# A two-block sequence model on one core: the residual stream held token-major instead of channel-major

## The chip, the cores and the metric

The kernel runs on one core of one Trainium2 chip, in a single launch. The metric is the device time of that launch in microseconds (us), lower is better. Runs of the kernel before the change took 2954.91, 2952.97 and 2952.49 us; their median is 2952.97 us.

## The reference

The input x has 512 tokens of 1024 channels in float32. Eight stages follow each other; every one takes the residual stream x, normalises it, computes a mixer or a feed-forward part of it, and adds the result to x:

```python
for i in range(2):                       # first block
    h = rmsnorm(x, norm_mix_pre[i])
    m = ssd_mixer(h, ...) if i == 0 else rglru_mixer(h, ...)
    x = x + rmsnorm(m, norm_mix_post[i])
    h = rmsnorm(x, norm_ffn_pre[i])
    x = x + rmsnorm(conv_ffn(h, ...), norm_ffn_post[i])
...                                      # second block: even mixer, ffn, latent attention, ffn
```

`rmsnorm(x, w)` is x * rsqrt(mean(x^2 over the 1024 channels) + 1e-6) * w, per token. `conv_ffn` is an up product, a causal depthwise convolution along the tokens, a gate and a product back to 1024 channels; its inner width is 4096 in the first block and 2816 in the second. `ssd_mixer` (state-space, 2048 inner channels), `rglru_mixer` (gated linear recurrence, 1280 channels), the even mixer (HGRN2 and S5) and latent attention also begin with a product from 1024 channels and end with a product back to 1024. The second block adds its results without the norm behind (its stages have no post norm), and a last rmsnorm gives the output.

## The kernel before

**Layout.** x lies in eight tiles of 128 channels x 512 tokens (`x[k]`, L351). A product takes the weights as the stationary operand (128 x 128) and 512 tokens as the moving one. All products are made of two-part float32r values: a weight chunk and an activation are each split into a high and a low part, and `mm3` (L394) issues three matmuls, high-high, high-low and low-high. One output tile of 1024 inputs ("a unit", one weight chunk of eight blocks) is 24 matmuls of 512 columns (`proj`, L403).

**Weights.** Chunks are loaded by SP (`Weights.load`, L252), cast to the high part (`wh`, ScalarE or VectorE, L277 and L279) and the low part is the difference (`wl`, VectorE or GpSimd, L280), ahead of use, into pools of six buffers each.

**Norms.** `Entry.put` (L478) makes x * gain in two parts, not yet divided by the rms. The 1/rms of each token is `R`: squares on ScalarE (L426, L429), their sum over eight tiles on VectorE or GpSimd, a matmul with a matrix of ones that sums over the partitions (`inv_rms`, L442, the matmul is L447), logarithm, exponential and a Newton step. R is a 128 x 512 tile, and each unit's result is multiplied by it when it is taken out of PSUM: `pa<-mm,R`, `pb`, `cp`, `z`, `u`, `pr`, `t` and others, all at L392 (the helper `tt`). Convolutions then read that padded copy (`conv`, L631: one ScalarE instruction L634, then two or three VectorE instructions L636).

**The ends of stages.** The last product of a stage is taken together with the start of the next one. `post_end` (L527) ends the four stages that have a post norm (ssd, ffn0, lru, ffn1): the last product in halves of 256 tokens, the squares, R of each half, `newx` (L547: x += acc * R * gain, then `nxt.put`), and the first three units of the next stage in the same halves. GpSimd takes part in it (`nx` at L392, and `wl`, since L533 sets the plan "ag"). `res_end` (L581) ends even, ffn2 and mla: each output tile is added to x and put at once, and units begin while later tiles come. `final_end` (L594) ends ffn3 with the last norm and the output. After an end, up to three further units are taken into other PSUM banks until R of the entry is there (`ent.norm`).

**What sets the order.** A tile scheduler orders the instructions of each engine when the program is built; engines then run their queues in that order. `Flow` (L296) interleaves the tasks of a mixer. PSUM has three banks "mm" for units, and per stage two to five banks "ax", three "dn" in the feed-forward stages, two "y" in ssd.

## Time and profile before

| | |
|---|---|
| median of 3 runs | 2952.97 us (2952.49 to 2954.91) |
| profiled execution: span, first to last instruction | 2949.6 us |
| that span below the median of the runs | 3.4 us |
| TensorE (PE) busy | 2857.2 us, 97% of the span |
| VectorE (DVE) | 2098.5 us, 71% |
| ScalarE (ACT) | 1302.7 us, 44% |
| GpSimd (POOL) | 570.7 us, 19% |
| mean granted TensorE clock | 0.987 |
| chain that ended last | 83% PE, 12% DVE, 2% ACT |

The profile is of one execution; the page gives no time for it but the span, so the table sets that beside the median. "Busy" of PE counts matmuls whose modelled ends overlap the next one's start, so a full PE shows 74.00 of 74 us. PEld is the load of the stationary operand, which runs beside the matmuls. [...]

### The profile page before, as it was taken

The numbers are of one execution on the slowest core, as the hardware profiler recorded it, in microseconds if no ns is written. First come the engines' busy times: TensorE is split into PE (matmuls) and PEld (weight loads), VectorE is DVE, ScalarE is ACT, GpSimd is POOL, SyncE is SP. The second block draws the span as 40 slices with busy tenths as digits, with TensorE's granted clock in tenths as the row PEclk, the third lists the DMA queues.
The fourth block names the chain that finished last, engine by engine and source line by source line (L and its number), as shares of the span: only waits on it lengthen the run. The fifth ranks groups of instructions, "written<-read, shape, count | busy, mean of one in ns | idle before, by whom it ended". The sixth has DMA issues, their size and how long they took to land.

```text
span 2949.6 us, 36037 instructions
## 1 busy us (share of the span) xinstructions
PE 2857.2 (97%) x13264; PEld 2312.0 (78%) x13264; DVE 2098.5 (71%) x3346; ACT 1302.7 (44%) x2166; POOL 570.7 (19%) x751
## 2 busy tenths in 40 slices
PE   9999989999999879899999999999999999999998
PEld 7777778888888767778888877887888876788887
DVE  8987788666666996797767776676555576765555
ACT  5444446444333464553343344554333354443333
POOL 1323233000000544512432443101000010100000
PEclk9999999999999999999999999999999999999999
DMA  5122132222222122233333335622222221122222
GB/s 179 58 72 72 58 113 74 100 99 87 100 100 88 70 72 89 70 104 111 116 122 121 123 112 162 196 75 98 100 87 99 100 75 33 68 100 96 90 100 72
DMA packets 100639, 284.73 MB, mean 97 GB/s; under 512 B 19568, under 2 KB 30320, under 8 KB 99952
## 3 DMA queue, kind: packets, MB, share of 16 engines
q1 hardware_dynamic: 89824, 271.13, 26.9%
q10 hardware_dynamic: 10640, 11.30, 1.2%
q8 instruction: 105, 1.72, 0.2%
q14 instruction: 70, 0.57, 0.1%
HBM read 266.19 MB, written 16.22 MB: 96 GB/s over the span
## 4 chain that ended last, share of the span: by engine, by line
PE 83%; DVE 12%; ACT 2%; issue 1%; POOL 1%; DMA 1%; SPq 0%; DVEq 0%; POOLq 0%; ACTq 0%
PE mm L397 18%; PE mm L396 18%; PE mm L398 18%; PE dn L396 7%; PE dn L398 7%; PE dn L397 7%; DVE S L392 2%; DVE xl L485 2%; DVE x L551 1%; DVE wl L280 1%; PE ax L1700 1%; DVE co L636 1%; PE y L843 1%; PE ax L447 1%; PE ax L1722 1%
## 5 line engine op out<-in xcount | busy, mean ns | idle before, releaser
L277 ACT CAST wh<-raw 128x512 fp32r<-128x512 f32 x886 | 545.0, 620 | 1057.0 <-PE mm L397 658.8
L396 PE MATMUL mm<-xh,wh 128*128 128x512 f32 (+1 forms) x2440 | 941.1, 388 | 28.3 <-ACT xh L484 19.6
L397 PE MATMUL mm<-xl,wh 128*128 128x512 f32 (+1 forms) x2440 | 943.2, 387 | 18.8 <-DVE xl L485 18.8
L398 PE MATMUL mm<-xh,wl 128*128 128x512 f32 (+1 forms) x2440 | 938.8, 385 | 0.7 <-DVE wl L280 0.7
L280 DVE TENSOR_TENSOR wl<-raw,wh 128x512 fp32r<-128x512 f32 x822 | 600.6, 733 | 162.6 <-ACT wh L277 155.7
L396 PEld LDWEIGHTS mm<-xh,wh 128*128 128x128 f32 x2440 | 463.3, 191 | 123.2 <-ACT xh L484 22.0
L397 PEld LDWEIGHTS mm<-xl,wh 128*128 128x128 f32 x2440 | 464.8, 191 | 117.0 <-DVE xl L485 27.2
L398 PEld LDWEIGHTS mm<-xh,wl 128*128 128x128 f32 x2440 | 465.4, 191 | 91.3 <-issue 1.8
L396 PE MATMUL dn<-hsh,wh 128*128 128x512 f32 (+1 forms) x912 | 350.6, 384 | 0.1
L398 PE MATMUL dn<-hsh,wl 128*128 128x512 f32 (+1 forms) x912 | 349.4, 383 | 0.0
L397 PE MATMUL dn<-hsl,wh 128*128 128x512 f32 (+1 forms) x912 | 349.3, 383 | 0.0
L280 POOL TENSOR_TENSOR wl<-raw,wh 128x512 fp32r<-128x512 f32 x114 | 164.2, 1450 | 237.4 <-ACT wh L277 128.9
L396 PEld LDWEIGHTS dn<-hsh,wh 128*128 128x128 f32 x912 | 171.3, 188 | 37.8 <-issue 0.9
L398 PEld LDWEIGHTS dn<-hsh,wl 128*128 128x128 f32 x912 | 171.3, 188 | 37.0
L397 PEld LDWEIGHTS dn<-hsl,wh 128*128 128x128 f32 x912 | 171.4, 188 | 36.9
L636 DVE SCALAR_TENSOR_TENSOR ca<-pa,vec,ca 128x512 f32<-128x512 f32 x216 | 173.8, 805 | 37.0 <-ACT ca L634 31.3
L641 POOL MEMSET pa<- 128x2 f32 x108 | 10.4, 99 | 741.0 <-DVE ca L636 524.8
L392 DVE TENSOR_TENSOR acc<-dn,acc 128x512 f32<-128x512 f32 (+1 forms) x144 | 90.1, 628 | 76.7 <-PE dn L398 76.5
L392 DVE TENSOR_TENSOR x<-dn,x 128x512 f32<-128x512 f32 (+1 forms) x104 | 67.5, 650 | 105.2 <-PE dn L398 105.1
L392 DVE TENSOR_TENSOR pa<-mm,R 128x512 f32<-128x512 f32 x104 | 71.7, 690 | 75.6 <-PE mm L398 73.9
L634 ACT ACTIVATE ca<-pa,vec 128x512 f32<-128x512 f32 x108 | 88.2, 816 | 56.3 <-DVE pa L392 46.7
L410 ACT CAST hsh<-act 128x512 fp32r<-128x512 f32 x108 | 66.9, 620 | 100.5 <-DVE act L392 100.5
(512 smaller groups left out, 3767.1 us busy)
## 6 DMA issues: line engine op xcount, KB each, us to landing
raw<-w SPq DMA_DIRECT2D x233, 1024.0 KB, 4.8
sD<-s5t SPq DMA_DIRECT2D x4, 1024.0 KB, 5.7
sR<-s5t SPq DMA_DIRECT2D x4, 768.0 KB, 4.4
x<-xT SPq DMA_DIRECT2D x8, 256.0 KB, 5.8
kept<-x SPq DMA_DIRECT2D x8, 256.0 KB, 8.5
xo<-kept ACTq DMA_DIRECT2D x8, 256.0 KB, 3.0
s5t<-el ACTq DMA_DIRECT2D x8, 256.0 KB, 2.2
s5t<-HD ACTq DMA_DIRECT2D x4, 512.0 KB, 3.2
```

The source lines that it names most:

```text
L277: c.nc.scalar.copy(hi, r)
L280: (c.nc.gpsimd if e[1] == "g" else c.nc.vector).tensor_tensor(lo, r, hi.bitcast(F32), op=ALU.subtract)
L392: (eng or V).tensor_tensor(o, a, b, op=op)
L396: PE.matmul(ps, lhsT=wh, rhs=xh, start=first, stop=False)
L397: PE.matmul(ps, lhsT=wh, rhs=xl, start=False, stop=False)
L398: PE.matmul(ps, lhsT=wl, rhs=xh, start=False, stop=last)
L410: A.copy(hi, src)
L447: PE.matmul(ps[:, sl], lhsT=ones, rhs=s[:, sl], start=True, stop=True)
L485: V.scalar_tensor_tensor(lo[:, sl], x[k][:, sl], gk, hi[:, sl].bitcast(F32), op0=ALU.mult, op1=ALU.subtract)
L551: V.scalar_tensor_tensor(x[k][:, sl], t[:, sl], vc(gpost, k), (xo or x)[k][:, sl], op0=ALU.mult, op1=ALU.add)
L634: A.activation(o, src[:, nt - 1:], AF.Identity, scale=w[nt - 1], bias=b)
L636: V.scalar_tensor_tensor(o, src[:, j:j + T], w[j], o, op0=ALU.mult, op1=ALU.add)
```

## The change

x is now four tiles of 128 tokens x 1024 channels (a block of tokens each). The products back to 1024 channels take the activations as the stationary operand and 512 columns of weights as the moving one (`mmt`), so that their results are token-major; a last product is taken block by block of tokens, not in halves. The norm is along the free axis: `rms_rows` is two ScalarE squares with an accumulated sum (L494) and two GpSimd instructions on one column (L496, L497, a power of -1/2). `Entry.put` scales x by 1/rms (`n`, L513), transposes it on TensorE (eight 128 x 128 transposes per block, L516), and makes the two parts with the gain from PSUM (L521 on ScalarE, L522 on VectorE, eight of each per block). What the units give is then normed already: the multiplications by R are gone, and convolutions read PSUM directly. All seven inner ends are one function, `stage_end`, which takes three units of the next stage in halves; the first stage starts in the same way. The gain of a post norm is a row loaded by SP (`row`, L399). The pool of split weights has seven buffers.

```diff
+        def rms_rows(src):
+            ss = small.tile([P, 2], F32, name="ss", tag="ss")
+            for h in range(2):
+                A.activation(tmp("sq"), src[h], AF.Square, scale=1.0 / 32, accum_out=ss[:, h:h + 1])
+            rr = small.tile([P, 1], F32, name="rr", tag="rr")
+            G.tensor_scalar(rr, ss[:, :1], ss[:, 1:], EPS, op0=ALU.add, op1=ALU.add)
+            G.tensor_tensor(rr, rr, mhalf, op=ALU.pow)
+            return rr
...
-            def put(self, k, sl=FULL, square=True):
...
+            def put(self, q):
+                rr = rms_rows([half(x, q, h) for h in range(2)])
+                qs = slice(q * P, q * P + P)
+                for h in range(2):
+                    n = tmp("n")
+                    A.activation(n, half(x, q, h), AF.Identity, scale=rr)
+                    ps = mmps(c.tp)
+                    for e in range(4):
+                        PE.transpose(ps[:, e * P:e * P + P], n[:, e * P:e * P + P], ident)
+                    for e in range(4):
+                        hi, lo = self.xs[4 * h + e]
+                        gk = vc(self.gain, 4 * h + e)
+                        pe = ps[:, e * P:e * P + P]
+                        A.activation(hi[:, qs], pe, AF.Identity, scale=gk)
+                        V.scalar_tensor_tensor(lo[:, qs], pe, gk, hi[:, qs].bitcast(F32),
+                                               op0=ALU.mult, op1=ALU.subtract)
...
+        def mmt(ps, hk, q, w, first, last):
+            (hh, hl), (wh, wl) = hk, w
+            qs = slice(q * P, q * P + P)
+            PE.matmul(ps, lhsT=hh[:, qs], rhs=wh, start=first, stop=False)
+            PE.matmul(ps, lhsT=hh[:, qs], rhs=wl, start=False, stop=False)
+            PE.matmul(ps, lhsT=hl[:, qs], rhs=wh, start=False, stop=last)
...
         def down(name, hs, acc, first=None):
...
+            for h in range(2):
+                ws = parts_of(name, n)
+                for q in range(4):
+                    ps = mmps(c.dn)
+                    for k in range(n):
+                        mmt(ps, hs[k], q, ws[k], k == 0, k == n - 1)
...
+            def newx(q):
+                if g is not None:
+                    rr = rms_rows([half(acc, q, h) for h in range(2)])
+                    for h in range(2):
+                        t = tmp("nx")
+                        V.scalar_tensor_tensor(t, half(acc, q, h), rr, g[h],
+                                               op0=ALU.mult, op1=ALU.mult)
+                        tt(half(x, q, h), t, xo[2 * q + h] if xo else half(x, q, h), ALU.add)
+                nxt.put(q)
+            dn(0)
+            dn(1)
+            newx(0)
+            dn(2)
+            newx(1)
+            dn(3)
+            newx(2)
             uc = [W.next(u) for u in units]
             up = [mmps() for _ in units]
...
+            units_half(uc, up, nxt.xs, 0)
+            newx(3)
+            units_half(uc, up, nxt.xs, 1)
...
         def conv(name, src, nt, w, b):
...
-            A.activation(o, src[:, nt - 1:], AF.Identity, scale=w[nt - 1], bias=b)
+            A.activation(o, src, AF.Identity, scale=w[nt - 1], bias=b)
             for j in range(nt - 1):
-                V.scalar_tensor_tensor(o, src[:, j:j + T], w[j], o, op0=ALU.mult, op1=ALU.add)
+                d = nt - 1 - j
+                V.scalar_tensor_tensor(o[:, d:], src[:, :T - d], w[j], o[:, d:], op0=ALU.mult, op1=ALU.add)
...
             def convd(ps, ch, nm):
-                pad = padded("p" + nm, 3)
-                tt(pad[:, 2:], ps, r)
-                return conv("c" + nm, pad, 3, [vc(cw, t * nch + ch) for t in range(3)], vc(cb, ch))
+                return conv("c" + nm, ps, 3, [vc(cw, t * nch + ch) for t in range(3)], vc(cb, ch))
...
-                        pad = tmp("cp", 3 + T)
-                        A.copy(pad[:, :3], lneg[:, 3 * h:3 * h + 3])
-                        tt(pad[:, 3:], ps, r)
-                        o = conv("co", pad, 4, [vc("lcw", NH * t_ + h) for t_ in range(4)], lcb[:, h:h + 1])
+                        o = conv("co", ps, 4, [vc("lcw", NH * t_ + h) for t_ in range(4)], lcb[:, h:h + 1])
+                        tt(o[:, :3], o[:, :3], less[:, h], ALU.subtract)
...
+                if n == 0:
+                    warm_up()
+                    W.look = 0
+                    for q in range(4):
+                        ent.put(q)
+                        if q == 1:
+                            uc = [W.next("sin") for _ in range(3)]
+                            pre = [mmps() for _ in uc]
+                            units_half(uc, pre, ent.xs, 0)
+                    units_half(uc, pre, ent.xs, 1)
```

The order of instructions moves at three places.

ScalarE at the end of ffn0, the change: one block of tokens (`acc_4324` is the result of the second block, `x_82` and `x_83` are the first two blocks of x, `xh_4301` and so on are the high parts for the next stage).

```order
L494 ACTIVATE sq,ss<-acc_4323 128x512 x2
L494 ACTIVATE sq,ss<-x_82 128x512 x2
L283 CAST wh<-raw 128x512
L513 ACTIVATE n<-x_82,rr 128x512 x2
L494 ACTIVATE sq,ss<-acc_4324 128x512
L521 ACTIVATE xh_4301<-ax,vec 128x128
L521 ACTIVATE xh_4309<-ax,vec 128x128
L494 ACTIVATE sq,ss<-acc_4324 128x512
L521 ACTIVATE xh_4303<-ax,vec 128x128
L521 ACTIVATE xh_4311<-ax,vec 128x128
```

Before, ScalarE had there one square of 256 tokens and one `xh` per channel tile and half. Now each block has four squares, two scalings and eight small `xh` in its queue, and the next block's squares stand between them.

TensorE at the end of the even mixer, the change (`n_16759` and `n_16774` are the two halves of the first block's normed x; `ax_16743` is a half of the second block's last product, `ax_16789` of the third's, and `hsh`, `hsl` are the activations).

```order
L535 MATMUL ax_16743<-wl_16716,hsh_16523 128x512
L536 MATMUL ax_16743<-wh_16715,hsl_16524 128x512
L516 MATMUL ax_16761<-ident_104,n_16759 128x128 x4
L516 MATMUL ax_16776<-ident_104,n_16774 128x128 x4
L534 MATMUL ax_16789<-wh_16671,hsh_16411 128x512
L535 MATMUL ax_16789<-wl_16672,hsh_16411 128x512
```

The transposes of a block stand in TensorE's queue ahead of the last product of a later block, so that product waits until the earlier block is normed.

VectorE in the LRU mixer, where two heads' convolutions are taken out of PSUM; before and then the change.

```order
L392 TENSOR_TENSOR cp<-mm,R 128x512
L657 SCALAR_TENSOR_TENSOR spp<-spp,spq 128x10
L392 TENSOR_TENSOR cp<-mm,R 128x512
L657 SCALAR_TENSOR_TENSOR spp<-spp,spq 128x10
L279 CAST wh<-raw 128x512
L657 SCALAR_TENSOR_TENSOR spp<-spp,spq 128x10
L636 SCALAR_TENSOR_TENSOR co<-cp,vec,co 128x512
```

```order
L633 SCALAR_TENSOR_TENSOR co<-mm,vec,co 128x509
L285 CAST wh<-raw 128x512
L633 SCALAR_TENSOR_TENSOR co<-mm,vec,co 128x510
L633 SCALAR_TENSOR_TENSOR co<-mm,vec,co 128x509
L633 SCALAR_TENSOR_TENSOR co<-mm,vec,co 128x511
L633 SCALAR_TENSOR_TENSOR co<-mm,vec,co 128x510
L411 TENSOR_TENSOR co<-co,less 128x3
```

The multiplication by R is gone, the three convolution instructions read the PSUM bank `mm` themselves, and a small correction of three columns is added.

## Rows read from the trace of the kernel before

**Rows 1.** The page: span, busy time of TensorE, and the chain that ended last.

```profile
span 2949.6 us, 36037 instructions
...
PE 83%; DVE 12%; ACT 2%; issue 1%; POOL 1%; DMA 1%; SPq 0%; DVEq 0%; POOLq 0%; ACTq 0%
```

**Rows 2.** Stretch, length, busy PE, PEld, DVE, ACT, POOL; clock, DMA share, GB/s.

```profile
5.80:27.60 21.80, 18.94 (x74) 13.29 (x75) 18.97 (x28) 17.52 (x29) 4.37 (x7) 1.00 0.93 330
30.00:421.00 391.00, 379.58 (x1853) 292.82 (x1852) 328.37 (x493) 176.45 (x290) 105.71 (x105) 1.00 0.22 74
...
592.00:666.00 74.00, 74.00 (x325) 60.76 (x324) 50.01 (x74) 30.70 (x47) 0.89 (x9) 1.00 0.29 100
966.20:1010.00 43.80, 36.40 (x246) 34.29 (x246) 40.52 (x74) 24.35 (x53) 25.05 (x24) 0.84 0.13 49
1010.00:1188.00 178.00, 157.84 (x645) 124.14 (x644) 139.91 (x201) 88.64 (x133) 85.06 (x59) 0.95 0.24 83
...
1992.60:2016.70 24.10, 22.12 (x97) 17.95 (x97) 12.50 (x15) 9.01 (x15) 6.48 (x7) 1.00 0.27 93
...
2927.00:2949.60 22.60, 12.75 (x101) 12.04 (x100) 17.97 (x47) 8.24 (x20) 0.00 (x0) 0.87 0.28 94
```

**Rows 3.** TensorE's timeline in the post end of ffn0: start, duration, instruction, idle before.

```profile
966.26 0.28 PE L396 MATMUL dn<-hsh,wh 128*128 128x256 f32 x1
...
977.97 0.28 PE L398 MATMUL dn<-hsh,wl 128*128 128x256 f32 x1
980.73 0.91 PE L396 MATMUL mm<-xh,wh 128*128 128x256 f32 x3 [2.48 <-ACT xh L484]
...
982.50 0.41 PE L398 MATMUL mm<-xh,wl 128*128 128x256 f32 x1
```

**Rows 4.** TensorE's timeline in the res end of the even mixer and behind it.

```profile
1999.80 0.50 PE L397 MATMUL mm<-xl,wh 128*128 128x512 f32 x1 [1.98 <-DVE xl L485]
...
2016.52 0.39 PE L398 MATMUL dn<-xh,wl 128*128 128x512 f32 x1
2016.75 1.02 PE L447 MATMUL ax<-S,ones 128*128 128x512 f32 x2
```

**Rows 5.** TensorE's waits (us, count, longest) in ssd, 30 to 421, then lru, 1010 to 1188.

```profile
PE y L843 <- DVE sc L392: 5.2, 5, 1.4
...
PE mm L396 <- DVE cp L392: 7.7, 3, 4.4
PE ax L396 <- ACT xbh L410: 5.9, 3, 2.9
```

**Rows 6.** Groups of VectorE by line, 1010 to 1188 us: count, busy us, mean ns.

```profile
L636 DVE SCALAR_TENSOR_TENSOR co<-cp,vec,co 128x512 f32<-128x512 f32 x30 | 26.5, 899 | 0.0
...
L392 DVE TENSOR_TENSOR t<-mm,R 128x512 f32<-128x512 f32 x10 | 6.6, 679 | 0.0
...
L392 DVE TENSOR_TENSOR S<-S,sq 128x512 f32<-128x512 f32 x3 | 4.4, 1455 | 0.8 <-ACT sq L429 0.6
```

**Rows 7.** Groups of the whole trace by line and shape: what the new instructions are nearest to.

```profile
L484 ACT ACTIVATE xh<-x,vec 128x256 fp32r<-128x256 f32 x64 | 32.5, 507 | 50.3 <-DVE x L551 49.0 <-DMA sa<-s5a 1.2
...
L429 ACT ACTIVATE sq<-x 128x512 f32<-128x512 f32 x51 | 30.4, 618 | 0.0
...
L862 DVE SCALAR_TENSOR_TENSOR yy<-xc,vec,y 128x512 f32<-128x512 f32 x16 | 11.8, 740 | 0.0
...
L1442 DVE SCALAR_TENSOR_TENSOR st<-st,pr,ax 128x128 f32<-128x128 f32 x24 | 8.3, 345 | 0.9 <-ACT st L1440 0.5
...
L1706 ACT ACTIVATION_READ_ACCUMULATOR p<-ax,mx 128x1 f32 x32 | 6.2, 195 | 0.0
```

**Rows 8.** Small two-input instructions of GpSimd (lines); four transposes (TensorE's timeline).

```profile
L392 POOL TENSOR_TENSOR u<-tc,us 128x16 f32<-128x16 f32 x4 | 3.3, 824 | 0.3
...
L392 POOL TENSOR_TENSOR u<-ts,us 128x8 f32<-128x8 f32 x4 | 0.8, 204 | 0.0
...
50.11 0.60 PE L768 MATMUL ax<-ident,B 128*128 128x128 f32 x4
```

More of the change, by code (lines that the diff above doesn't have):

```diff
@@ L381, in build, with half, row @@
         FULL = slice(0, T)
+        def half(a, q, h):
+            return a[q][:, h * T:h * T + T]
+        def row(n):
+            out = [tmp("row") for _ in range(2)]
+            for h in range(2):
+                nc.sync.dma_start(out[h], aps["rows"][n:n + 1, h * T:h * T + T].to_broadcast([P, T]))
+            return out
         def tmp(name, w=T, dt=F32):
@@ L505, in down, with parts_of @@
+        def parts_of(name, n):
+            out = []
+            for _ in range(n // 2):
+                out += W.next(name).halves
+            return out
         def down(name, hs, acc, first=None):
             n = len(hs)
-            per = 8 // n
-            for j in range(KD):
-                if j % per == 0:
-                    ch = W.next(name)
-                ps = mmps(c.dn)
-                proj(ps, ch, hs, k0=(j % per) * n)
-                if first is None:
-                    tt(acc[j], ps, acc[j], ALU.add)
-                else:
-                    first(acc[j], ps, j)
-                yield n * 0.65, 0.0
@@ L520, in copy_first @@
-        def copy_first(a, ps, j):
+            for h in range(2):
+                ws = parts_of(name, n)
[3 more added lines that the diff above has]
+                        mmt(ps, hs[k], q, ws[k], k == 0, k == n - 1)
+                    if first is None:
+                        tt(half(acc, q, h), ps, half(acc, q, h), ALU.add)
+                    else:
+                        first(half(acc, q, h), ps, h)
+                    yield n * 0.69, 0.0
```

377 lines of the change are left out of this document (128 added, 249 removed).

## The prediction

> **What bounds the kernel now.** I read the page first, for the span, the busy shares and the chain that ended last [rows 1]: 83% of that chain is TensorE. Then the busy time by stretch [rows 2], because an average hides where TensorE is not full. In ffn0 it is busy 74.00 of 74 us at clock 1.00 while VectorE is busy 50.01: work taken off VectorE or ScalarE is worth nothing there, and this holds in all feed-forward stages. The reader should compare the other lines with it. ssd: TensorE lacks 391.00 - 379.58 = 11.4 us. lru: 178.00 - 157.84 = 20.2 us, and the clock is 0.95, another 178 x 0.05 = 9 us. A post end: 7.4 us of 43.8, at clock 0.84. A res end: 2.0 of 24.1. The output: TensorE is busy 12.75 of 22.6 us, so about 9.9 pass without it. What it waited for comes last: in lru mostly `cp` of VectorE and `xbh` of ScalarE, in ssd `sc` of VectorE [rows 5].
>
> So the change can gain in the interiors of ssd and lru and at the output, and can gain or lose at the start and at the seven ends between stages. The number of matmuls in the products stays what it is; 256 transposes come and the matmuls with `ones` go. The sum is made against the profiled span of 2949.6 us [rows 1], which is 3.4 below the median of the runs, 2952.97.
>
> **A post end, four times.** Before, it takes 43.8 us up to the first full-width unit [rows 2], and the norm's matmul between units costs about 1 us more [rows 4]: 44.8. In the change ScalarE gets a chain of small work for each block of 128 tokens: four squares with a sum, two scalings, eight `xh`. A 512-wide square takes 0.618 and a read of the accumulator 0.195 [rows 7]: 4 x 0.81 = 3.3. A scaling is taken like the square: 2 x 0.62 = 1.2. An `xh` of 128 columns isn't in the trace; it lies between the 128x1 at 0.195 and the 128x256 at 0.507 [rows 7]; I take 0.35, in between by width, so 2.8. That is 7.3 a block and 29 for four. Some five weight casts in the same queue, priced like the square, add 3. The queue begins when the first block's last product is done, a quarter of 11.7 us [rows 3], about 2.7 in. What it waits for is the chain of the first and of the last block: two pairs of GpSimd instructions on one column, VectorE's update of x, four transposes (0.60 [rows 8]). A 128x8 instruction of GpSimd takes 0.204 and a 128x16 one 0.824 [rows 8]; I take 0.4, nearer to the smaller since a column is smaller still, so 0.8 a pair; with 1.4 for VectorE (two of about 0.7) and the transposes that is 3.6, exposed about once and a half: 5. The last `xh` is then out at 2.7 + 29 + 3 + 5 = 40. The first halves of the three units lie before that, beside ScalarE. Behind it come `xl` (0.345, like the 128x128 instruction of VectorE [rows 7]), the last block's matmuls of the first unit, and two unit halves: 48 matmuls of 256 columns, whose pitch I take as half of a 512-column one. 72 of those and two more fill 18.9 us at the start [rows 2], hence 0.24, and half is 0.12: 5.8. After an idle of 2.48 us the trace shows such matmuls at 0.41 instead of 0.28 [rows 3], and clock 0.84 for the stretch, so some of the 48 will run at the lower clock: 2. End: 40 + 0.8 + 5.8 + 2 = 48.6, against 44.8: **+4 each, +16**. Bounds: all at full clock and the chain hidden gives 44 (-1); 0.824 for each GpSimd instruction adds 0.8 to each pair, and TensorE at the low clock throughout adds 4: 56 (+11).
>
> [...]
>
> **A res end, three times.** Before: 24.1 us hold the last product and two units [rows 2]; a third unit (24 matmuls at 22.1 / 97 = 0.23 us [rows 2]: 5.5) and the norm's matmul (1.0) make 30.6. In the change ScalarE has two squares less a block, 5.7, so 23 for four blocks and 2.5 for four casts. It begins at a quarter of the last product (2.7) and one VectorE addition (0.7): last `xh` at 29, the end at 29 + 0.8 + 5.8 = 35.6, so +5 each; since `xl` and the first unit's last matmuls run beside ScalarE's next ones I take 4.4, **+13**. Bounds: +1 (ScalarE's small instructions overlapping) and +9 (low clock, slow GpSimd).
>
> **The start.** Before, units begin as soon as a tile of x has come, and 74 matmuls are done at 27.6 [rows 2], with the DMA queues 0.93 full at 330 GB/s. Now nothing can begin before a whole block (0.5 MB instead of 0.25, 0.8 us later) is normed, and the second halves wait for four times 5.7 = 23 us of ScalarE and some casts (2): 5.85 + 0.8 + 23 + 2 + 0.8 + 5.8 = 38: **+10**. Bounds +5 and +15. **The output** loses about 9.9 us without TensorE to a chain of one block (two squares 1.6, a pair 0.8, one VectorE instruction 0.75, the transfer): some 6, so **-4**, bounds -6 and 0.
>
> **lru.** VectorE loses ten `cp` and ten `t` at 0.68 (13.6 us), the sums `S` (4.4 and more [rows 6]) and the contention that they suffer: `co` takes 0.899 there, while the instruction of the same kind that reads PSUM takes 0.740 (L862, [rows 7]), 30 x 0.16 = 4.8. It gains ten corrections of three columns (0.16 each, the price of the accumulator read as a bound) and the bias of the last product, eight at 0.69: 7. Net 16 us of 139.9. The waits named in [rows 5] end on just this work or on work queued behind it, and the norm is gone at the entry. Of the 20.2 us idle and 9 at the low clock I take **-18**; bounds -29 (all of it) and -6 (the next wait, ScalarE's `xbh`, comes in its place).
>
> **ssd** loses 24 `cp` and 16 `z` of the same shape, 27 us of VectorE's 328; the waits that these can shorten are 11.4 at most: **-8**, bounds -11 and 0. Even and latent attention lose the same multiplications; I count nothing, since TensorE's queue covers VectorE there, and allow -5. The feed-forward stages: nothing; TensorE covers 50 of 74 us and the change only takes from it. A unit's PSUM bank is now held for a ScalarE pass and two VectorE instructions (0.62 + 2 x 0.74 = 2.1 us) instead of one of 0.68, of the 16 that three banks allow.
>
> [...]
>
> **Sum.** 16 + 13 + 10 - 4 - 18 - 8 = +9 on 2949.6, or 2958; with 3.4 for the median **about 2961**.
>
> **Rivals.** (A) *Faster*: the ends keep up, since small instructions on ScalarE overlap their neighbours. Post ends 0, res ends +1.5 each, start +6, output -5, lru -25, ssd -11: 2949.6 - 30 + 3.4 = 2923. For it speaks that TensorE's and VectorE's own work at the ends falls; against it that ScalarE's queue at a post end rises from 24 us of work [rows 2] to 32. It decides if the last `xh` of a post end is out before 35 us. (B) *Much slower*: the power on GpSimd costs like 0.824 or more, and each end's second halves run at the low clock. Post ends +11, res ends +8, start +14, output -2, mixers -20: 2949.6 + 60 + 3.4 = 3013. (C) *Even*: ends and interiors cancel, within some 6 us of 2953. (D) *The mixers keep their waits*: the convolutions read PSUM at 0.90 (the rate of `co`) and hold the banks, lru and ssd give -10 together: 2977.
>
> **Chances.** 0.2% is about what a measurement of this kernel can tell from no change, 6 us here. The forecast 0.30, A 0.36, C 0.16, B 0.12, D 0.06. The forecast, B and D are slower: faster 0.36, same 0.16, slower 0.48. The likeliest sign is slower, and the forecast is the middle of that side; for it alone I give 2956 to 2975. The range leaves out the far end of A and most of B: 2919 to 3000.
>
> **What would show it.** Post ends of 47 to 50 us with TensorE waiting for `xh` right before the second halves; res ends near 35; the third unit of ssd done near 38 us; GpSimd pairs of 0.8; lru without waits for `cp` and `t` and its stretch 15 to 20 us shorter; the last matmul 6 us before the end. The forecast is wrong if the ends are as long as before (ScalarE's 128-column instructions then cost nearer 0.25), or if lru's stretch hardly moves (its bound is then not VectorE).

## The result and the profile after

The change is slower: 2988.97 us (median of four runs, 2987.97 to 2990.36) against 2953.94 for the kernel before, measured beside it; the ratio is 1.0121, with a 95% interval of 1.0107 to 1.0135. The sign and the range of the prediction held. The forecast size did not: +9 us on the span, and the profiled span went from 2949.6 to 2988.6, +39.

The page of the changed kernel, its span, the engines' busy time and the chain that ended last:

```profile
span 2988.6 us, 35753 instructions
...
PE 2870.8 (96%) x13528; PEld 2347.7 (79%) x13528; DVE 1878.0 (63%) x3120; ACT 1291.0 (43%) x2366; POOL 416.6 (14%) x524
...
PE 86%; DVE 7%; ACT 4%; POOL 2%; issue 1%; DMA 1%; SPq 0%; DVEq 0%; POOLq 0%; ACTq 0%
```

VectorE lost 220 us of work and GpSimd 154, and the kernel became slower: neither was the bound in most stages. TensorE shows 2870.8 us where it had 2857.2. The stretches answer to [rows 2]; columns as there.

```profile
0.00:43.30 43.30, 31.07 (x198) 29.84 (x199) 20.21 (x48) 28.58 (x70) 8.28 (x24) 0.80 0.44 159
...
434.70:489.90 55.20, 39.03 (x226) 34.93 (x225) 34.28 (x73) 33.63 (x86) 7.40 (x16) 0.81 0.14 49
500.00:900.00 400.00, 400.00 (x1762) 330.38 (x1761) 235.10 (x339) 161.02 (x259) 0.00 (x0) 1.00 0.27 95
986.50:1042.10 55.60, 37.85 (x225) 33.67 (x225) 38.50 (x98) 31.62 (x82) 13.35 (x21) 0.85 0.13 43
1042.10:1206.80 164.70, 157.24 (x660) 126.87 (x661) 122.08 (x177) 69.64 (x98) 88.35 (x55) 0.97 0.27 95
1206.80:1268.40 61.60, 41.93 (x225) 37.30 (x224) 33.39 (x81) 33.69 (x87) 17.52 (x32) 0.78 0.15 53
1775.70:1831.00 55.30, 39.47 (x225) 35.70 (x224) 34.51 (x80) 32.63 (x86) 7.71 (x18) 0.81 0.25 89
2015.70:2050.90 35.20, 33.42 (x225) 29.45 (x224) 23.60 (x54) 26.73 (x69) 3.45 (x8) 1.00 0.17 60
2977.90:2988.60 10.70, 0.15 (x1) 0.00 (x0) 4.36 (x7) 2.06 (x6) 1.72 (x4) 0.66 0.39 145
```

They are, from the top: the start, the post end of ssd, a piece of ffn0, the post end of ffn0, lru, the post ends of lru and ffn1, the res end of even, and what follows the last matmul. An end is counted here from the first matmul of the last product to the first full-width unit of the next stage (at the res ends, to the fourth unit), and the stretches between them fill the span. The two traces side by side, all of them taken from TensorE's timeline:

| stretch | before | after | difference |
|---|---|---|---|
| start, three units done | 27.6 | 43.4 | +15.8 |
| ssd | 394.1 | 391.4 | -2.7 |
| post ends of ssd, ffn0, lru, ffn1 | 43.5, 43.7, 43.2, 43.6 | 55.2, 55.6, 61.6, 55.3 | +53.7 |
| ffn0 and ffn1 | 501.2, 511.0 | 496.7, 507.2 | -8.3 |
| lru | 182.6 | 164.7 | -17.9 |
| even | 191.1 | 184.7 | -6.4 |
| res ends of even, ffn2, mla | 29.9, 33.1, 29.9 | 35.2, 35.2, 35.2 | +12.8 |
| ffn2 and mla | 336.0, 180.9 | 332.9, 179.7 | -4.2 |
| ffn3 and the output | 358.5 | 354.7 | -3.8 |

They add up to +39. The old norm's matmul behind the first units, about 1 us each time, which the prediction counted with the ends, lies in the stretch behind them here. Taken off the ends it leaves +50 for the post ends (forecast +16) and +10 for the res ends (forecast +13).

What TensorE waited for over the whole span (us, times, longest) names the new bound:

```profile
PE ax L516 <- ACT n L513: 51.8, 17, 8.7
PE y L516 <- ACT n L513: 19.9, 4, 9.1
PE mm L417 <- POOL wl L286: 7.5, 3, 5.3
PE y L516 <- DVE xl L522: 6.0, 2, 3.3
PE y L828 <- DVE sc L411: 4.4, 4, 1.8
```

77.7 us are waits of the transposes (L516), nearly all for the scaled block `n` of ScalarE. Yet ScalarE is not full at the post ends: 31.6 us busy of 55.6 in the one of ffn0, just the 32 that the prediction had summed. Its queue there shows why (ScalarE's timeline between the scalings of the first block and those of the second: start, duration, instruction, and in brackets the idle time before and what ended it):

```profile
997.07 1.34 ACT L513 ACTIVATE n<-x,rr 128x512 f32<-128x512 f32 x2 [0.56 <-POOL rr L497]
998.31 0.61 ACT L494 ACTIVATE sq<-acc 128x512 f32<-128x512 f32 x1
...
999.48 0.62 ACT L494 ACTIVATE sq<-acc 128x512 f32<-128x512 f32 x1
...
1003.23 0.63 ACT L494 ACTIVATE sq<-x 128x512 f32<-128x512 f32 x1 [0.29 <-DVE x L411]
...
1005.55 0.63 ACT L494 ACTIVATE sq<-x 128x512 f32<-128x512 f32 x1 [1.60 <-DVE x L411]
...
1007.35 1.33 ACT L513 ACTIVATE n<-x,rr 128x512 f32<-128x512 f32 x2 [1.07 <-POOL rr L497]
1008.59 0.61 ACT L494 ACTIVATE sq<-acc 128x512 f32<-128x512 f32 x1
```

The squares of the second block's result (`sq<-acc`, 998.31) stand behind the first block's scalings (`n`, 997.07); the third block's stand behind the second's (1008.59 behind 1007.35). So the chain of a block, squares, GpSimd pair, update of x on VectorE, squares again, pair, scaling, begins only when that of the block before is through: 10.3 us from one `n` to the next, of which ScalarE works 7.3. TensorE sees it as one long gap between the transposes of the first block and of the second:

```profile
998.58 0.60 PE L516 MATMUL ax<-ident,n 128*128 128x128 f32 x4
...
1008.12 1.97 PE L516 MATMUL ax<-ident,n 128*128 128x128 f32 x8 [8.48 <-ACT n L513]
```

At the end of lru, whose last product is otherwise the same, TensorE's queue adds to it. There the transposes of the first two blocks stand ahead of the products of the third and fourth, which could have run in the gaps (its timeline):

```profile
1212.20 0.40 PE L536 MATMUL ax<-wh,hsl 128*128 128x512 f32 x1
1218.31 1.97 PE L516 MATMUL ax<-ident,n 128*128 128x128 f32 x8 [5.71 <-ACT n L513]
...
1229.79 1.97 PE L516 MATMUL ax<-ident,n 128*128 128x128 f32 x8 [5.23 <-ACT n L513]
```

### The profile page after: what moved, and what is told of

Its sections match the earlier page's. It is cut to its first block, busy times and chain, and to the rows that moved or that the text cites. A ratio compares the mean times of both kernels' runs of the same rounds, so it can differ in the third digit from the quotient of the medians.

```text
span 2988.6 us, 35753 instructions
## 1 busy us (share of the span) xinstructions
PE 2870.8 (96%) x13528; PEld 2347.7 (79%) x13528; DVE 1878.0 (63%) x3120; ACT 1291.0 (43%) x2366; POOL 416.6 (14%) x524
## 4 chain that ended last, share of the span: by engine, by line
PE 86%; DVE 7%; ACT 4%; POOL 2%; issue 1%; DMA 1%; SPq 0%; DVEq 0%; POOLq 0%; ACTq 0%
PE mm L415 18%; PE mm L416 17%; PE mm L417 17%; PE dn L535 6%; PE dn L534 6%; PE dn L536 6%; PE mm L534 2%; PE mm L535 2%; PE mm L536 2%; ACT sq L494 1%; ACT n L513 1%; DVE wl L286 1%; POOL rr L497 1%; PE ax L1656 1%; PE ax L1678 1%
## 5 line engine op out<-in xcount | busy, mean ns | idle before, releaser
L286 DVE TENSOR_TENSOR wl<-raw,wh 128x512 fp32r<-128x512 f32 x870 | 633.8, 735 | 501.2 <-ACT wh L283 485.4
L534 PE MATMUL dn<-wh,hsh 128*128 128x512 f32 x864 | 339.3, 393 | 2.6 <-DVE acc L411 2.6
L535 PE MATMUL dn<-wl,hsh 128*128 128x512 f32 x864 | 340.7, 394 | 0.3 <-DVE wl L286 0.3
L536 PE MATMUL dn<-wh,hsl 128*128 128x512 f32 x864 | 335.8, 389 | 0.0
L496 POOL TENSOR_SCALAR rr<-ss 128x1 f32<-128x1 f32 x52 | 16.3, 314 | 1554.8 <-ACT sq L494 1554.7
L534 PEld LDWEIGHTS dn<-wh,hsh 128*128 128x128 f32 x864 | 162.2, 188 | 41.0 <-DVE acc L411 3.0
L536 PEld LDWEIGHTS dn<-wh,hsl 128*128 128x128 f32 x864 | 162.2, 188 | 35.9
L535 PEld LDWEIGHTS dn<-wl,hsh 128*128 128x128 f32 x864 | 162.5, 188 | 32.9 <-DVE wl L286 0.7
L633 DVE SCALAR_TENSOR_TENSOR ca<-mm,vec,ca 128x510 f32<-128x510 f32 x216 | 161.6, 748 | 16.1 <-ACT ca L630 12.5
L411 DVE TENSOR_TENSOR acc<-dn,acc 128x512 f32<-128x512 f32 x128 | 87.6, 686 | 83.7 <-PE dn L536 83.4
L633 DVE SCALAR_TENSOR_TENSOR cb<-mm,vec,cb 128x510 f32<-128x510 f32 (+1 forms) x128 | 95.7, 748 | 9.8 <-ACT cb L630 7.9
L630 ACT ACTIVATE ca<-mm,vec 128x512 f32<-128x512 f32 x108 | 83.8, 776 | 11.3 <-PE mm L417 11.3
```

What stands on the lines that cost most here:

```text
L286: (c.nc.gpsimd if e[1] == "g" else c.nc.vector).tensor_tensor(lo, r, hi.bitcast(F32), op=ALU.subtract)
L411: (eng or V).tensor_tensor(o, a, b, op=op)
L534: PE.matmul(ps, lhsT=hh[:, qs], rhs=wh, start=first, stop=False)
L535: PE.matmul(ps, lhsT=hh[:, qs], rhs=wl, start=False, stop=False)
L536: PE.matmul(ps, lhsT=hl[:, qs], rhs=wh, start=False, stop=last)
L630: A.activation(o, src, AF.Identity, scale=w[nt - 1], bias=b)
```

## The experiments

Three theories for the post ends: (1) the order in ScalarE's queue makes the chains of the blocks follow one another; (2) the amount of work, of ScalarE or in the chain, sets the pace whatever the order; (3) the low clock of TensorE behind its waits (0.81, 0.85, 0.78 and 0.81 in the mean at these ends) does. The figures are from the profile of each run; its span lies 1.7 to 2.8 us below its time. Every run here but `combined` was timed once. Where two runs have the same order, their post ends agree within 0.5 us, and ffn0 between its ends takes 496.7 us in eight of them; but the start scatters from 41.0 to 43.4 us among the runs that leave it alone, and the change's 43.4 is the longest.

### Squares one block ahead, and all products first

An earlier start of the squares needs a little more on-chip memory, so it ran with six weight buffers, beside a control that has the six buffers and nothing else (`WSP = 6`).

> The change with six buffers of split weights instead of seven, which frees 4 KB for the runs that need it. All theories: the span of the change, 2988.6 us, within 3 us, and the four post ends as in it (55.2, 55.6, 61.6 and 55.3 us from the first matmul of the last product to the first full-width unit).

Measured: span 2998.1, so six buffers cost 9.5 us, which no theory had. The post ends were 54.0, 55.6, 61.7 and 53.7; the loss lay between the ends: lru 167.1 (164.7 with seven), ffn1 510.6 (507.2), even 189.1 (184.7), mla 180.9 (179.7).

```diff
             dn(0)
+            r0 = pre(0)            # the squares and the pair of a result
             dn(1)
-            newx(0)
+            r1 = pre(1)
+            newx(0, r0)            # update of x and put
             dn(2)
-            newx(1)
+            r2 = pre(2)
+            newx(1, r1)
             dn(3)
-            newx(2)
+            r3 = pre(3)
+            newx(2, r2)
```

> The squares of a block's result and its first GpSimd pair are written one block ahead, so that in ScalarE's queue they stand ahead of the previous block's two scalings and not behind them; no work is added or removed (six weight buffers). Theory 1, the post ends are long because each block's chain starts only behind the previous block's scalings in ScalarE's queue (10.2 us a block, of which ScalarE works 7.3): two squares with their sums (1.6) and a GpSimd pair (0.95) leave the chain of three blocks, so each post end is 6 to 9 us shorter and the span 25 to 36 shorter, about 2958. Theory 2, ScalarE's amount of work or the other steps of the chain (VectorE's update of x, the second pair, the transposes) set the pace: post ends shorter by 0 to 2 us, span 2980 to 2989. Theory 3, the low clock sets it: the waits shrink but the last halves stay at 0.41 a matmul, 2 to 4 us an end. Res ends, start and interiors: unchanged in all.

Measured: span 2980.5, 17.6 below the control. Post ends 45.2, 49.6, 57.4 and 46.3, that is 8.8, 6.0, 4.3 and 7.4 shorter; res ends 35.3, 35.8 and 35.2. Theory 1 holds at three of four ends, and theory 2, which gave at most 2, falls. The ends gained 26.5 in all, and the span less than the 25 to 36 expected, since stretches behind them grew: ffn0 by 2.8, ffn3 by 2.0, ffn2 by 1.9, ffn1 by 1.5. And one gap was left untouched, that between the transposes of the first two blocks at ffn0's end:

```profile
990.28 1.27 PE L516 MATMUL ax<-ident,n 128*128 128x128 f32 x8 [0.36 <-ACT n L513]
1000.35 1.97 PE L516 MATMUL ax<-ident,n 128*128 128x128 f32 x8 [8.80 <-ACT n L513]
1008.41 0.60 PE L516 MATMUL ax<-ident,n 128*128 128x128 f32 x4
```

The transposes of the third and fourth blocks now come 8.1 and 5.8 us behind those of the block before, where it was 9.9 and 9.8 in the change; those of the second still wait 8.80. The other edit moves only the products:

```diff
             dn(1)
-            newx(0)
             dn(2)
-            newx(1)
             dn(3)
+            newx(0)
+            newx(1)
             newx(2)
```

> All four blocks of the last product are written ahead of the first block's update; ScalarE's work is unchanged and its squares still stand behind the scalings. In TensorE's queue this moves the transposes of the first two blocks behind the last product at the end of lru and at the res ends, and hardly changes the other three post ends. If the end of lru is 6 us longer than the other post ends because the products of blocks 3 and 4 wait behind transposes in TensorE's queue (6.1 and 5.6 us idle there), it falls from 61.6 to about 55 and the span by 6. If it is longer because of its own chain (an addition more, VectorE), it stays at 60 or more. Ends of ssd, ffn0 and ffn1: within 1 us of the change. Res ends: 35.2 plus or minus 2.

Measured: the end of lru fell from 61.6 to 54.8, as TensorE's queue order would have it. The others did not all stay: ssd 57.5, ffn0 56.3, ffn1 55.7, and the res end of ffn2 went from 35.2 to 42.8, where the transposes now waited 6.3 us in one piece for `xl` of VectorE. So the span rose to 2993.5: the order that helps one end spoils another.

> Both edits: all four products, and the squares of all four results, stand ahead of the first block's scalings. Theory 1: post ends of 45 to 48 us, the end of lru like the others, span 2947 to 2958. Theory 2: post ends of 53 to 55 and a span of 2978 to 2985, of which 6 come from the end of lru alone. Theory 3: 51 to 53 each. At the res ends the first block's transposes stand behind the whole product: 0 to 2 us longer each.

Measured: 2998.1, no better than its control. Post ends 50.1, 54.1, 51.9 and 50.3, so 18.5 less than the control's in all; but the res ends took 37.0, 42.1 and 36.8, 9.7 more, and the stretches behind the ends grew by some 10. Only the end of lru was best so. At the other three, all squares of results now stood in ScalarE's queue ahead of the first block's squares of x, and these ends were 4 to 5 us longer than with the squares one block ahead. That they came near theory 3's 51 to 53 is no sign of the clock: the granted clock at the end of ssd is 0.83, with 0.81 in the change. No theory had given a span as long as this one.

### The chosen order at each end, and VectorE's queue

> The squares one block ahead as in the earlier run, but with seven weight buffers as in the change (the two small tiles of a sum and its root are one tile now, which frees the room), and at the end of lru all four products ahead of the first update. Theory 1 (the post ends wait in ScalarE's queue): post ends of about 45, 49, 52 and 46 us, as measured apart with six buffers, and lru, ffn1, even and latent attention between the ends as in the change (164.7, 507.2, 184.7 and 179.7): 2988.6 less 10, 6, 10 and 9 is about 2954. Rival: if the 9.5 us that six buffers cost came from something else than the buffers, the interiors stay as with six and the span is near 2965.

Measured: span 2958.3. Post ends 45.4, 48.9, 51.2 and 47.0; lru 165.0, ffn1 508.2, even 185.0, mla 181.1. These four interiors are within 1.4 us of the change's again, so the loss of the control did come from the missing seventh buffer. What is left of the 4 us above the expected 2954 has another source in part: the clock record of this run (0.936 in the mean, 0.985 in the next run) reads 0.95 where TensorE is full, and 1.00 in the others (600 to 900 us, where it issues 1318 matmuls and in the next run 1321), and stretches that no edit touches are some 1 us longer (ffn0 497.9 in place of 496.7, ffn2 334.5 in place of 332.9).

```diff
+            upd(0, a0)             # x += acc * rr * gain, VectorE
+            b0 = xs_(0)            # squares of x and the pair
             dn(2)
+            a2 = pre(2)
+            upd(1, a1)
+            put(0, b0)             # scaling, transposes, xh, xl of block 0
+            b1 = xs_(1)
             dn(3)
+            a3 = pre(3)
+            upd(2, a2)
+            put(1, b1)
+            b2 = xs_(2)
...
```

> As early_seven, and further: the update of x and the squares of x of a block are written ahead of the scalings and transposes of the block before it, so that on VectorE the update no longer stands behind eight xl of the previous block. If what is left of the chain is the order in VectorE's queue (9 us without TensorE between the transposes of the first and the second block in early_squares), post ends fall by 3 to 6 us more each, to about 42 to 44, and the span to 2935 to 2945. If ScalarE's work is what is left (32 us of it at a post end, and 12 us of products and matmuls that it can't cover), they fall by 0 to 1 us. Res ends within 2 us of 35.2.

Measured: span 2943.3. Post ends 42.0, 46.4, 45.9 and 43.2, res ends 36.2, 39.8 and 36.1. Against early_seven that is 3.4, 2.5, 5.3 and 3.7 less at the post ends: the order in VectorE's queue was a further part of the chain. (The spans differ by 15.0, some 8 of which lie between the ends, where early_seven was slower.) The res end of ffn2 missed what was expected, by 2.6 us. TensorE's timeline at the end of ffn0 shows where it left:

```profile
984.96 1.27 PE L517 MATMUL ax<-ident,n 128*128 128x128 f32 x8 [1.44 <-ACT n L514]
991.18 1.97 PE L517 MATMUL ax<-ident,n 128*128 128x128 f32 x8 [4.96 <-ACT n L514]
```

6.2 us from the first block's transposes to the second's, where it was 9.5 in the change and 10.1 with the squares alone moved. Between the scalings of the first block (984.19) and of the second ScalarE now works without a gap; three of the rows:

```profile
985.42 0.62 ACT L494 ACTIVATE sq<-x 128x512 f32<-128x512 f32 x1
...
987.15 0.62 ACT L494 ACTIVATE sq<-acc 128x512 f32<-128x512 f32 x1
...
990.39 1.35 ACT L514 ACTIVATE n<-x,ss 128x512 f32<-128x512 f32 x2
```

### What single parts cost

```diff
-            G.tensor_scalar(rr, ss[:, :1], ss[:, 1:], EPS, ...)
+            G.tensor_scalar(rr, ss[:, :1], ss[:, 1:], EPS, ...)
+            G.tensor_scalar(rr, ss[:, :1], ss[:, 1:], EPS, ...)
             G.tensor_tensor(rr, rr, mhalf, op=ALU.pow)
```

> The change with the first GpSimd instruction of each pair issued twice (0.30 us and a gap of 0.08). Theory 1, at a post end each block's chain runs one behind the other: eight pairs lie in it, so each of the four post ends is 2 to 3.5 us longer and the span 8 to 14 longer. If ScalarE's amount of work set the pace there, the pairs lie beside it and a post end grows by under 1. Res ends, where ScalarE is busy 26.7 of 35.2 us: under 1 each.

Measured: span 3000.1, 11.5 longer. The post ends grew by 4.0, 3.1, 2.2 and 0.9, the res ends by 0.6, 1.5 and 0.6, and the start was 1.9 shorter. Eight times 0.38 is 3.0, the mean of the four is 2.6: at the post ends most of the pairs lie in the chain one behind the other, and not beside a pace that ScalarE's amount of work sets. The single ends scatter more than the estimate, and the 0.9 of ffn1 is left open. The start holds the same pairs and became no longer; its 41.5 is within its scatter.

```diff
-                        PE.transpose(ps[:, e * P:e * P + P], n[...], ident)
+                        for _ in range(2):
+                            PE.transpose(ps[:, e * P:e * P + P], n[...], ident)
```

> Each of the 256 transposes is issued twice, to the same place. A transpose took 0.109 us back to back at the high clock, 32 at an end: 3.5 us. Theory P, the transposes lie on TensorE's path at the res ends, which have hardly any idle time (33.4 of 35.2 us busy): each res end 3 to 3.5 us longer. At the post ends, where TensorE waits for ScalarE's chain, 1 to 3.5 each at either clock; start 1 to 3; the span about 15 to 25 longer. Rival, the transposes lie in waits everywhere: under 1 us at each end, span within 6.

Measured: span 2998.3, 9.7 longer. Res ends +1.9, +2.4 and +1.9, start +3.6, post ends -0.1, +0.5, -3.3 and +0.1. At the res ends a little over half of the 3.5 us of transposes was on TensorE's path, between theory P and its rival; at the post ends nothing was, since TensorE waits there anyway (why the end of lru came out shorter is left open). The clock did not suffer from more transposes: the four post ends show 0.85, 0.88, 0.85 and 0.85, against 0.81, 0.85, 0.78 and 0.81 in the change.

```diff
-                        o = conv("co", ps, 4, ...)
+                        pad = tmp("cp")
+                        V.tensor_copy(pad, ps)
+                        o = conv("co", pad, 4, ...)
...
                         if q == 1:
                             uc = [W.next("sin") for _ in range(3)]
                             pre = [mmps() for _ in uc]
-                            units_half(uc, pre, ent.xs, 0)
+                        if q > 0:
+                            units_half(uc[q - 1:q], pre[q - 1:q], ent.xs, 0)
```

> Two edits of the change in stretches far apart. In lru each of the ten convolutions reads a copy that VectorE makes from PSUM (ten copies of about 0.68 us, 6.8 in all). Theory V, lru is bound by VectorE's work, so the 17.9 us that it gained are the multiplications and sums taken from VectorE: lru between its ends goes from 164.7 to 169 to 172 us. Rival: the gain came from the norm behind the first units and the low clock after it, and VectorE has room: 164 to 166. At the start, the first halves of the three units are written one behind each further block instead of all three behind the second, so that the transposes of blocks 3 and 4 no longer wait in TensorE's queue behind all of them (ScalarE idle from 26.1 to 29.1 us). If that order is why the start is 43.4 and not the 38 that ScalarE's work gives, it falls to 36 to 39; if it is the clock or the transfers, it stays at 42 or more.

Measured: lru went from 164.7 to 172.3, +7.6, as theory V said (169 to 172), and VectorE's busy time there from 122.1 to 140.0. The ten copies are only 6.8 of those 17.9 us, and some 3 are convolutions that lie just ahead of this stretch in the change. The thirty instructions of the convolution took 7.8 more than there; VectorE's groups in lru of this run:

```profile
L633 DVE SCALAR_TENSOR_TENSOR co<-cp,vec,co 128x509 f32<-128x509 f32 x10 | 13.5, 1354 | 0.0
...
L633 DVE SCALAR_TENSOR_TENSOR co<-cp,vec,co 128x511 f32<-128x511 f32 x10 | 8.4, 842 | 0.0
L633 DVE SCALAR_TENSOR_TENSOR co<-cp,vec,co 128x510 f32<-128x510 f32 x10 | 7.8, 781 | 0.0
```

and in the change, where the same instruction reads PSUM:

```profile
L633 DVE SCALAR_TENSOR_TENSOR co<-mm,vec,co 128x511 f32<-128x511 f32 x9 | 6.5, 734 | 0.0
L633 DVE SCALAR_TENSOR_TENSOR co<-mm,vec,co 128x510 f32<-128x510 f32 x9 | 6.5, 733 | 0.0
L633 DVE SCALAR_TENSOR_TENSOR co<-mm,vec,co 128x509 f32<-128x509 f32 x8 | 5.7, 728 | 0.4 <-ACT co L630 0.4
```

The mean over the three is 992 ns in this run and 732 in the change, but neither source is slower by itself. Of the 30 that read the copy, 22 took 719 to 745 ns, as those that read PSUM do (716 to 747). The other 8 took 1179 to 1778, and each of them began while GpSimd was at work on a `wl`. Of those that read PSUM three began so too, and took 731 to 747. One of each kind, first reading the copy (the second of the two, from 1067.29, took 1778 ns) and then PSUM in the change:

```profile
1066.63 2.44 DVE L633 SCALAR_TENSOR_TENSOR co<-cp,vec,co 128x511 f32<-128x511 f32 x2
1067.14 1.38 POOL L286 TENSOR_TENSOR wl<-raw,wh 128x512 fp32r<-128x512 f32 x1 [6.68 <-PE mm L416]
```

```profile
1067.41 1.29 POOL L286 TENSOR_TENSOR wl<-raw,wh 128x512 fp32r<-128x512 f32 x1 [0.72 <-DVE wh L285]
1067.56 0.73 DVE L633 SCALAR_TENSOR_TENSOR co<-mm,vec,co 128x509 f32<-128x509 f32 x1
```

An instruction that the edit leaves alone and that reads on-chip memory only (`gt<-gt,co`, L985) went from 676 to 1007 ns in the mean, 3.3 us in all.

At the start, the same run has three units done at 38.3 instead of 43.4; beside the scatter of the start, the order is worth 2.7 to 5 us. ScalarE's timeline there, first of the change and then of this run, has the cause:

```profile
24.71 1.34 ACT L513 ACTIVATE n<-x,rr 128x512 f32<-128x512 f32 x2 [0.31 <-POOL rr L497]
29.06 3.15 ACT L521 ACTIVATE xh<-y,vec 128x128 fp32r<-128x128 f32 x8 [3.02 <-PE y L516]
```

```profile
29.11 3.17 ACT L521 ACTIVATE xh<-y,vec 128x128 fp32r<-128x128 f32 x8 [0.88 <-PE y L516]
```

In the change these eight `xh`, at 29.06, belong to the third block, and eight more follow; in the run with the other order the ones at 29.11 are the last. The third block's transposes had stood in TensorE's queue behind the first halves of all three units.

### The parts together

The pipelined order at the post ends, the change's own at the res ends, and the other start:

```diff
+            if g is None:
+                dn(0); dn(1); put(0); dn(2); put(1); dn(3); put(2)
+            else:
+                ...                # as in pipelined
```

> The order of the run pipelined at the four post ends, the change's own order at the three res ends (where the pipelined order cost 0.9, 4.6 and 0.9 us), and at the start the first halves of one unit behind each further block (5.0 us in lru_copied). If these stretches are independent, the profiled span of pipelined, 2943.3, falls by 11 to about 2932, below the kernel before (2949.6) by 0.6%. Rival: what a stretch gains is given back in the next one, because split weights are not ready sooner (1 to 3 us were given back so behind the ends of early_squares): 2936 to 2941.

Measured in five runs: 2934.53 us (2934.36 to 2936.36) against 2953.77 for the kernel before in nine; the ratio is 0.994, interval 0.9927 to 0.9954, so small but clear of no change. The span is 2932.8, as the sum of the stretches gave, so hardly anything was given back. It has the token-major layout of the change, every instruction of it, and is faster than both kernels. It also has the change's seven buffers of split weights, worth 9.5 us above, where the kernel before has six; what a seventh would give that kernel was not tried, so the 0.6% is not shown to be the layout's alone. Its post ends and the first res end:

```profile
428.20:470.70 42.50, 35.48 (x226) 31.79 (x225) 34.45 (x72) 32.91 (x86) 10.14 (x16) 0.88 0.19 62
967.30:1014.00 46.70, 37.71 (x225) 33.53 (x224) 38.89 (x98) 31.29 (x82) 17.14 (x21) 0.85 0.16 51
1179.30:1225.20 45.90, 36.98 (x225) 32.54 (x224) 35.54 (x80) 32.51 (x86) 19.92 (x31) 0.85 0.20 69
1732.40:1775.50 43.10, 35.36 (x225) 31.72 (x224) 34.47 (x80) 32.17 (x86) 10.31 (x18) 0.88 0.31 110
1960.00:1995.20 35.20, 33.42 (x226) 29.46 (x225) 23.62 (x54) 26.73 (x69) 3.45 (x8) 1.00 0.18 60
```

ScalarE is busy as long as in the change (32.9 against 33.6 us at the end of ssd, 31.3 against 31.6 at that of ffn0) in 9 to 16 us less. The line of waits that led the list is down to a half, `n` at 25.6 us:

```profile
PE ax L517 <- ACT n L514: 25.6, 13, 6.1
PE y L517 <- DVE xl L523: 9.0, 3, 5.5
```

One more place was left, the output:

```diff
             for q in range(4):
                 dn(q)
-                outs(q)
+                if q:
+                    outs(q - 1)
+            outs(3)
```

> The run combined, with the output of a block written behind the next block's last product, so that on VectorE the last addition to x stands between the two scalings of the block before it and no longer behind both. In the change the last matmul is followed by 10.7 us; the last addition waits 1.4 us behind those scalings. If that order is why the output did not get shorter, 10.7 falls to 9 to 9.8. If the chain of the last block alone makes it up, it stays at 10.4 or more.

Measured: from the start of the last matmul to the end 9.7 us, where it was 11.0 in combined and in the change (10.7 from a little later on, as in the window above). The last matmul came 0.8 later, so of the 1.3 only 0.5 is left in the span, 2932.3; that is less than single runs differ by.

## Why the prediction was right or wrong

The sign held for the reason given: the ends and the start lose more than the mixers gain. That the time lies in the range, though above the 2956 to 2975 given for the forecast alone, is partly luck, for errors cancelled: the post ends cost 34 us more than forecast, the start, ssd and the output some 15 together, and stretches that were counted as nothing gave 17 back.

**The post ends, +16 forecast, +50 measured: the step that failed.** Its sum was right in its amounts: ScalarE's work (32 us forecast, 31.6 to 33.7 measured), the start of its queue (2.7 us in; the first square stands at 989.23, 2.7 behind 986.5), and the tail behind the last `xh` (8.6 forecast; the last ends at 1032.9, 9.2 before the first full-width unit, of which 2.1 are a wait for VectorE's `co`, which reads a unit's PSUM bank). One quotient in it is off, without harm: 18.9 us by 74 matmuls is 0.26, not 0.24; half units measure 0.122 a matmul, which gives the 5.8 that it used. What was wrong is "exposed about once and a half: 5". The chain was counted as if blocks overlapped, which ScalarE's queue does not allow: the squares of each block's result stand behind the scalings of the block before, so the chain is exposed at every block. From 989.2 to 1032.9 are 43.7 us in place of 37: less the 29 and 3 of work that leaves 12 of waits instead of 5. The excerpt of ScalarE's order that stands ahead of the prediction showed it: `sq` of the second block's result behind `n` of the first. It was read as work in the queue, not as a wait. Moving those instructions and those of VectorE, with none added or taken away, gave back 9 to 16 us at each post end. At the end of lru the order of TensorE's queue added 6 to 7 us; the text ahead of the prediction had named it at the res ends (the second excerpt), where the other order proved no better, and not there.

**The clock.** The forecast had 2 us at each post end for matmuls at the low clock, and rival B much more. In the traces of the two kernels the record of the granted clock has two levels, 1.00 and 0.50 (0.50 from 981 to 991 us in that of before, from 1005 to 1015 in the change); the matmuls of half units are issued every 0.12 us at the upper and every 0.21 at the lower. The mean did fall: it is 0.78 to 0.85 at the four ends, and was 0.84 at that of ffn0 [rows 2] and 0.88 at the other three. These before:

```profile
421.60:465.10 43.50, 35.32 (x246) 33.06 (x245) 36.51 (x67) 24.33 (x53) 24.69 (x24) 0.88 0.17 62
1192.60:1235.80 43.20, 34.83 (x245) 32.85 (x244) 36.64 (x69) 24.41 (x54) 25.95 (x31) 0.88 0.12 40
1746.80:1790.40 43.60, 35.13 (x245) 32.72 (x245) 37.96 (x72) 24.28 (x53) 27.40 (x27) 0.88 0.31 109
```

This is not the main cause of the long ends. At the end of ffn0 it did not fall (0.84 and 0.85), TensorE works 10.2 us at the lower level where it was 10.8, and the end is as much longer as those of ssd and ffn1. At the other three it works 12 to 19 us at the lower level, before 7 to 8. Eight transposes take 1.97 us at the lower level and 1.04 at the upper, so about half of the difference is a bound for what it costs, an estimate of 2.5 to 5.5 us each; part of it is hidden in waits, which no run sets apart. Combined, with shorter waits, shows 0.85 to 0.88. At three ends more idle time of TensorE and a lower mean went together, 8.2 to 8.5 us at 0.88 before and 15.8 to 19.7 us at 0.78 to 0.81 in the change; at that of ffn0 they did not, 7.4 us at 0.84 and 17.8 at 0.85. With twice as many transposes (transposes_twice) the clock at the post ends was a little higher (0.85 to 0.88), not lower.

**The res ends, +13 forecast, about +10 measured.** The amounts held: 35.2 us in place of the 35.6 forecast, three times, and at the end of even the last `xh` is out at 29.2 where 29 was forecast. That is in part luck, for the sum has ScalarE's chain alone: TensorE itself is busy 33.4 of the 35.2 us (the product, 32 transposes and 144 half matmuls), and the last eight `xh` wait 1.35 us for transposes that stand behind 72 half matmuls. The working has an error that did not carry into its sum: the 24.1 us of [rows 2] do not hold "the last product and two units" but four units, the product lies ahead of them; with the product (11 us), three units and the norm's matmul, the end before still is 30.9, or 34 for ffn2, which the prediction took as 30.6.

**The start, +10 forecast, +16 measured.** The 43.4 is the longest of the starts with this order (41.0 to 43.4), so +13 to +16. The sum by ScalarE's work, 38, was right for the order that the lru_copied run gives it (38.3). The change's order has the third block's transposes behind 64 matmuls, and ScalarE idle for 3.0 us and again behind. That is the same kind of mistake as at the post ends: a queue's amount was summed, its order not.

**lru, -18 forecast, -17.9 measured** (about 1 us of it the old norm's matmul), and, as far as it was tried, for the reason given: VectorE's work, 140.6 us before and 122.1 after in the stretches between the ends. TensorE's idle time fell from 20.2 to 7.5 us, and the waits for `cp`, `t`, `xbh` and `xbl` are gone; the next wait is not `xbh`, as the prediction's bound had it, but GpSimd's `wl` (7.0 of the 7.5). Copies back into the path cost 7.6. What the other 10 us come from (the products `t`, the sums `S`, the norm) was not tried apart.

**ssd, -8 forecast, -2.7 measured.** Its term assumed that waits go with the work taken off. `sc` on VectorE, 5.2 us of waits before [rows 5], still holds TensorE for 4.4, with VectorE at 308 of 391 us. The order around it was left open.

**The interiors counted as nothing** gave 23 us together, some 6 of which are the old norm's matmuls that the prediction had put to the ends. In ffn0 a further part is the product itself: 400 us hold 1762 matmuls in the change and 1749 before. The mean step from one matmul of the products back to the next is 0.2289 us now and 0.2332 before, from the starts of 672 such matmuls in each trace; the units' is 0.2267 in both. 672 times 4.3 ns is 2.9 us of the 4.5 that ffn0 lost. Whether the stationary operand makes the difference or something else that changed with it was not tried. This was not predicted; [rows 2] only said that TensorE is full there, not that its matmuls could come faster.

**The output, -4 forecast, 0 measured.** From the start of the last product's last matmul to the end are 11.0 us, before 10.8. The chain is one block's as forecast, but the last addition to x stands on VectorE behind two scalings of the block before; output_late took 1.3 us of it away.

**The rivals.** D has the nearest time (2977), but its mechanism did not happen: the convolution reads PSUM at 0.73, not 0.90, and lru and ssd gave 20.6 together, not 10. B (3013) had the length of the post ends (+11), but not its cause: the GpSimd pair takes 0.95 us, not twice 0.82, and the end of ffn0 grew by as much without a fall of the clock. A's post ends of about 44 are what combined shows (42.5 to 46.7), but not by A's mechanism: ScalarE works as long as in the change there, and its last `xh` is out at 36 to 41 us, not before 35. The convolution in lru was not slower for reading PSUM: it took 716 to 747 ns, against 719 to 745 from the copy where no `wl` of GpSimd ran as it began, and in the mean 732 ns from PSUM and 992 from the copy.

## What to carry to other kernels

When work is cut into blocks that each pass through four engines, add up each queue's amount, and then read its order for one block after another: what of block q+1 stands behind an instruction of block q that itself waits? Here the whole difference between 1.2% slower and 0.6% faster than before was that order, at the post ends and at the start, with the same instructions. Write the early steps of the next block ahead of the late steps of this one by one block, not by all, and try the order at each place by itself, since one that helps one end spoiled another.

## What the runs showed of the hardware

VectorE's convolution with one operand in PSUM and one in on-chip memory took 716 to 747 ns, also where it began beside a running GpSimd `wl`; with both operands in on-chip memory it took 719 to 745, and 1179 to 1778 in the eight cases where it began so. The products back issue a matmul every 0.2289 us with activations as the stationary operand, against 0.2332 with weights; the two kernels differ there in more than that. The 128x1 GpSimd instructions took 0.30 (two additions) and 0.56 us (the power). The 128x128 instructions of ScalarE took 0.37 alone, two in a row 0.61 and eight in a row 3.15, so 0.25 to 0.39 from one to the next, where 0.35 was forecast. A weight buffer fewer cost 9.5 us of 2989, most of it in lru, ffn1 and even.
